# Tiles moved to SBUF places at multiples of 512 bytes, and two merge buffers made one, in a two-layer diffusion step

## Chip, core and metric

One core of a Trainium2 chip runs the whole program. The metric is the device time of one execution in microseconds (us). One execution of the kernel before was also taken by the profiler; all rows of a profile below are of that one.

## What is computed

One inference step of a small diffusion backbone with two layers, in float32. It works on 640 tokens of width 1024: 128 context tokens and 512 latent tokens (a grid of 8 x 64). Cut to what matters here:

```python
for l in range(2):
    hp = rmsnorm(xp, norm1_g[l]) * (1 + sc1p) + sh1p          # 128 context tokens
    hs = rmsnorm(xs, norm1_g[l]) * (1 + sc1s) + sh1s          # 512 latent tokens
    if l == 0:   # gated DeltaNet: projections q, k, v, z, a chunked scan both ways, w_out
        mp, ms = gdn_mixer(hp, ...), gdn_mixer(hs, ...)
    else:        # neighbourhood attention over the grid and over cached context keys, w_out
        mp, ms = context_attention(...), neighbourhood_attention(...)
    xp, xs = xp + g1p * mp, xs + g1s * ms
    xp = xp + g2p * conv_ffn(rmsnorm(xp, norm2_g[l]) * (1 + sc2p) + sh2p, ...)
    xs = xs + g2s * conv_ffn(rmsnorm(xs, norm2_g[l]) * (1 + sc2s) + sh2s, ...)
y = rmsnorm(x, final_g)

def conv_ffn(h, w_up, conv_w, conv_b, w_down):
    val, gate = split(dwconv_centred(h @ w_up, conv_w) + conv_b)   # 1024 -> 2 * 2816
    return (silu(gate) * val) @ w_down                             # 2816 -> 1024
```

The shifts, scales and gates come from `silu(c) @ w_ada + b_ada` for each layer.

## The kernel before

**Layout.** Features lie on the 128 partitions, tokens along the free dimension. The residual `X`, the normalized input of a product `hh`/`hl`, and each feature tile of the ConvFFN are rows of W = 640 float32 values, 2560 bytes per partition, the context tokens first.

**The products.** Every large product is made of three matmuls per block of 128 x 128 weights (`pass3`, L405): operand and weight are each split into a part rounded to the type float32r ("hi": `hh`, `wh`) and the rest ("lo": `hl`, `wl`), and hi·hi (L410), lo·hi (L411) and hi·lo (L412) are summed in PSUM. The moving operand is 384 columns wide, and then the other 256 (`HALVES_U`, `HALVES_R`); in the DeltaNet's projections the second part has 260 columns and begins 4 columns earlier (`HALVES_G`). A matmul with its weight load is one entry of the profile's engine PE and one of PEld. The names of the products: `dg`, `dkT`, `dqT`, `dvT`, `dzs` are the DeltaNet's projections, `rgo` its output projection, `duv` and `dug` the two halves of the up-projection, `rdn` the down-projection (its moving operand is `F`), `dqn`, `dkn`, `dvn` the attention's projections, `rne` and `rno` its output projection (its moving operand is `A`).

**The weights.** `weights` (L381) loads a chunk of weights (128 partitions x 4096 bytes for eight blocks) into one of two staging tiles `wst` by a DMA of the SyncE queue; `split` (L387) casts it on ScalarE into `wh` (L398) and subtracts on VectorE, or on GpSimd in the DeltaNet part, into `wl` (L400). `wh` and `wl` have two places each in the pool `wp`; some chunks are kept longer in places of their own.

**Order of the stages.** A start (modulation of layer 0, norm, first projections); the DeltaNet, in the order of the string `SCHED`; its output projection; the ConvFFN of layer 0, with the other modulations between its products (`ada_tile`, L154: matmuls L163 on four column groups, and L173 with a moving operand of two columns); the attention, one pair of heads after another, with the next projections between its steps; its output projection; the ConvFFN of layer 1 with the final norm. The Tile framework orders the instructions by priorities in the program and sets every wait.

**SBUF.** Tile pools are stacked: the place of a pool is the sum of the sizes of those opened before it that are still open, each tile rounded up to 32 bytes. `cst` lies lowest and holds the constants, `hh`, `hl`, the modulations and a few small tiles, some of which are allocated late in the program (`sel` at L129, `mods` at L139, `scg` at L285, `UT` and `LT` at L626, `half` at L1044). On it lies `wp` (`wst`, `wh`, `wl`), on that `gs` (small tiles of the DeltaNet), on that first the pools of the start, then `gp` (all other tiles of the DeltaNet), and when `gs` and `gp` are closed `X` and the pools of all that follows. The places before, in bytes along a partition, and the remainder by 512:

| tile | begins at | remainder by 512 |
|---|---|---|
| `hh`, `hl` | 19936, 40416 | 480 |
| `wst` (2) | 64032, 68128 | 32 |
| `wh`, `wl` (2 each) | 72224 ... 84512 | 32 |
| `X` after the DeltaNet | 88608 | 32 |
| tiles of `gp`, first `kT` | 90848 | 224 |
| `A` (8), `F` (9) | 118816 ..., 129056 ... | 32 |
| softmax tiles `P` (4) | 183456, 184960, 186464, 187968 | 160, 128, 96, 64 |

Second parts of the moving operand (256 columns) begin 1536 bytes behind the row's start, three times 512; the 260 columns begin 1520 bytes behind it, at remainder 464. A block of weights begins at a multiple of 512 bytes within its chunk, a feature row at a multiple of 2560, five times 512.

**The merge** (`merge`, L849), once for each of the eight heads, joins inverted 32 x 32 blocks: matmuls `p1`, copied to the tile `P1` by ScalarE (L880), `p2` and `p3` that read `P1`, copies back (L890, L894), `p4`, copied to `P4` (L903), `p5` that reads `P4`, and a copy back (L909). `W6`, `Wx`, `P1` and `P4` have one buffer each.

Of the kernel before, what the change touches and what calls it, by code (L numbers as in the profile page):

```python
# [12 lines left out]
F32 = mybir.dt.float32  # L13
# [13 lines left out]
NBLK = 5  # L27
# [22 lines left out]
LO0 = (1, 1, 0)  # L50
HK, HK2 = (6, 11), (2, 5)
TAB = 4
ADL, NPOOL = 1, 10
GROUPS = ((0, 8), (8, 15), (15, 22))

# [28 lines left out]
class Net:  # L84
    def __init__(self, ctx, tc, a):
        self.ctx, self.tc, self.nc, self.a = ctx, tc, tc.nc, a
        nc = self.nc
        self.cst = ctx.enter_context(tc.tile_pool(name="cst", bufs=1))
        self.lo_engine = nc.vector
        self.pd = self.pa = None  # L90
        self.wide = False
        self.hooks, self.strict = [], False
        self.chain = False
        self.pooled = None
        self.product = None
        self.wp = ctx.enter_context(tc.tile_pool(name="wp", bufs=2))
        cst = self.cst
        self.sm = cst.tile([128, NSM], F32, tag="sm", name="sm")
        nc.sync.dma_start(self.sm, a["sm"])
        self.ident = cst.tile([128, 128], F32, tag="ident", name="ident")  # L100
        make_identity(nc, self.ident)
        self.ones = cst.tile([128, 128], F32, tag="ones", name="ones")
        nc.vector.memset(self.ones, 1.0)
        self.mhalf = cst.tile([128, 8], F32, tag="mhalf", name="mhalf")
        nc.vector.memset(self.mhalf, -0.5)
        self.eps = cst.tile([128, 1], F32, tag="eps", name="eps")
        nc.vector.memset(self.eps, EPS)
        self.X = None
        self.hh = cst.tile([128, KT, W], F32R, tag="hh", name="hh")
        self.hl = cst.tile([128, KT, W], F32R, tag="hl", name="hl")  # L110
        self.cs = cst.tile([128, KT, 32], F32, tag="cs", name="cs")
        nc.vector.memset(self.cs, 0.0)
        self.mods = [None, None]
        self.scg = {}

    def open_x(self, pool):
        self.X = pool.tile([128, KT, W], F32, tag="X", name="X")
# [8 lines left out]

    def ada_begin(self):
        nc, cst = self.nc, self.cst
        self.sel = cst.tile([128, 2], F32, tag="sel", name="sel")  # L129
        nc.vector.tensor_copy(self.sel, self.ident[:, 0:2])  # L130
        for q in range(1, 4):
            nc.vector.tensor_tensor(self.sel, self.sel, self.ident[:, 32 * q : 32 * q + 2], ALU.add)
        nc.scalar.activation(
            self.cs[:, :, 0:2], self.smv("c").rearrange("p (k v) -> p k v", v=2), AF.Silu
        )
# [143 lines left out]
    def scale_vec(self, l, which, ks=range(KT)):  # L279
        nc = self.nc  # L280
        base = 8 if which == 1 else 32
        lo, hi = min(ks), max(ks) + 1
        g = self.smv("n1g" if which == 1 else "n2g").rearrange("p (l k) -> p l k", l=2)[:, l]
        if (l, which) not in self.scg:
            self.scg[l, which] = self.cst.tile([128, 8, 2], F32, tag=f"scg{l}{which}", name=f"scg{l}{which}")  # L285
        nc.vector.scalar_tensor_tensor(
            self.scg[l, which][:, lo:hi],
            self.mods[l][:, base + lo : base + hi, :],
            1.0,
            g[:, lo:hi].unsqueeze(2).to_broadcast([128, hi - lo, 2]),  # L290
            ALU.add,
            ALU.mult,
        )
# [60 lines left out]

    def norm_tile(self, np_, rs, half, k, l, which):
        nc = self.nc
        if (l, which) not in self.scg:
            self.scale_vec(l, which)
        scg = self.scg[l, which]
        base = HALVES_R[half][0]  # L360
        for hf, c0, c1, v in SEGS:
            if hf != half:
                continue
            n = c1 - c0
            t = np_.tile([128, 256], F32, tag="nt", name=f"nt{l}{which}{k}{c0}", bufs=3)
            nc.vector.scalar_tensor_tensor(
                t[:, :n], self.X[:, k, c0:c1], scg[:, k, v : v + 1], rs[:, c0 - base : c1 - base], ALU.mult, ALU.mult
            )
            sh = self.mod(l, 0 if which == 1 else 3, k, v)
            nc.scalar.activation(self.hh[:, k, c0:c1], t[:, :n], AF.Identity, bias=sh)  # L370
            nc.vector.scalar_tensor_tensor(  # L371
                self.hl[:, k, c0:c1], t[:, :n], sh, self.hh[:, k, c0:c1].bitcast(F32), ALU.add, ALU.subtract
            )
# [230 lines left out]
class Gdn:  # L604
# [17 lines left out]
    def tokens(self):  # L622

        net, nc, a = self.net, self.nc, self.net.a
        cst = net.cst
        self.UT = cst.tile([128, 128], F32, tag="UT", name="UT")  # L626
        self.LT = cst.tile([128, 128], F32, tag="LT", name="LT")
        for t, sgn in ((self.UT, 1), (self.LT, -1)):
            nc.gpsimd.affine_select(
                out=t, in_=net.ones, pattern=[[sgn, 128]], compare_op=ALU.is_ge, fill=0.0, base=0,  # L630
# [218 lines left out]
    def merge(self, h, yd, wd):  # L849
# [22 lines left out]
        def mm(out, lhsT, rhs, r, c):  # L872
            nc.tensor.matmul(out, lhsT, rhs, start=True, stop=True, tile_position=(r, c))

        p1 = self.g(f"p1{h}")
        for d, qa, qb in quads:
            for u in range(NBLK):
                mm(p1[b32(qb), u * 32 : u * 32 + 32], M[b32(qa), d, u, b32(qb)], wa[qa](u), 32 * qa, 32 * qb)
        P1 = self.gp.tile([128, NBLK, 32], F32, tag="P1", name=f"P1{h}", bufs=1)
        nc.scalar.copy(P1, p1[:, : NBLK * 32].rearrange("p (u c) -> p u c", c=32))  # L880
        p2 = self.g(f"p2{h}")
        for d, qa, qb in quads:
            for u in range(NBLK):
                mm(p2[b32(qa), u * 32 : u * 32 + 32], P1[b32(qb), u], M[b32(qb), d, u, b32(qb)], 32 * qb, 32 * qa)
        p3 = self.g(f"p3{h}")
        for d, qa, qb, o in ((0, 0, 1, 0), (1, 3, 2, 32)):
            for u in range(NBLK):
                mm(p3[b32(qb), u * 32 : u * 32 + 32], M[b32(qb), d, u, b32(qb)], P1[b32(qb), u], 32 * qb, 32 * qb)
        for d, qa, qb in quads:
# [12 lines left out]
        P4 = self.gp.tile([128, NBLK, 64], F32, tag="P4", name=f"P4{h}", bufs=1)  # L902
# [138 lines left out]

    def tokens_(self):
        net, nc = self.net, self.nc
        self.half = net.cst.tile([128, NBLK], F32, tag="half", name="half")  # L1044
        nc.vector.memset(self.half, 0.5)
        self.tokens()

# [444 lines left out]
def build(ctx, tc, a):  # L1492
# [32 lines left out]
    with tc.tile_pool(name="fp0", bufs=2, reuse_waits="tile") as fp:  # L1525
# [20 lines left out]
        def between(i):  # L1546
            if i is not None and i >= TAB:
                with net.behind([net.load]):
                    next(rows, None)
            if i is not None:  # L1550
                if joins:
                    joins.pop()()
                if direct:
                    joins.append(net.ada_tile(*direct.pop(0), fp, 1, 3, True, nxt.pop()))
                    if direct:
                        nxt.append(load())
            if calls[0] > 1:
                with net.behind([net.pooled]):
                    next(beside, None)
            calls[0] += 1  # L1560
            if i == NFT - 1:
                run(beside)
                assert not direct and not joins
# [104 lines left out]
```

## Time and profile before

| | us |
|---|---|
| median of 3 runs | 1960.89 |
| the runs | 1957.93 to 1971.5 |
| the profiled execution | 1957.87 |
| its span, from the first instruction to the last | 1955.8 |
| mean granted TensorE clock | 0.976 |

How to read it: each row of a timeline is one instruction or a run of alike ones, with its start and its duration. Matmuls are pipelined, so a row's duration is longer than the time until the next one starts; the pace of a stream is the distance from start to start, not the duration. Rows by line group the instructions of one source line; the part behind the last bar is the idle time of the engine ahead of them and what ended it.

### The profile page before, as it was taken

The numbers are of one execution on the slowest core, as the hardware profiler recorded it, in microseconds if no ns is written. First come the engines' busy times: TensorE is split into PE (matmuls) and PEld (weight loads), VectorE is DVE, ScalarE is ACT, GpSimd is POOL, SyncE is SP. The second block draws the span as 40 slices with busy tenths as digits, with TensorE's granted clock in tenths as the row PEclk, the third lists the DMA queues.
The fourth block names the chain that finished last, engine by engine and source line by source line (L and its number), as shares of the span: only waits on it lengthen the run. The fifth ranks groups of instructions, "written<-read, shape, count | busy, mean of one in ns | idle before, by whom it ended". The sixth has DMA issues, their size and how long they took to land.

```text
span 1955.8 us, 34936 instructions
## 1 busy us (share of the span) xinstructions
PE 1866.7 (95%) x14047; PEld 1762.7 (90%) x14047; DVE 1162.4 (59%) x2708; ACT 723.7 (37%) x1455; POOL 432.7 (22%) x436
## 2 busy tenths in 40 slices
PE   6889999999989999999999999999999999999998
PEld 5878888887869999999999998888889999999998
DVE  6687657767666665356446565554576643553564
ACT  4453344343334332133124344444454421331343
POOL 1332113121201828477620111111130000000000
PEclk9889899999899999999999999999999999999999
DMA  7223123323314445255233232222241322222231
GB/s 286 72 79 104 44 94 110 92 52 130 91 58 161 139 153 171 88 165 182 77 115 102 63 90 76 78 78 72 60 128 46 88 75 66 85 80 64 86 97 55
DMA packets 100835, 193.16 MB, mean 99 GB/s; under 512 B 38744, under 2 KB 58282, under 8 KB 97528
## 3 DMA queue, kind: packets, MB, share of 16 engines
q1 hardware_dynamic: 96544, 175.99, 29.0%
q0 software_dynamic: 3584, 14.40, 2.3%
q8 instruction: 111, 1.82, 0.4%
q10 hardware_dynamic: 544, 0.52, 0.1%
q14 instruction: 52, 0.43, 0.1%
HBM read 182.04 MB, written 12.46 MB: 99 GB/s over the span
## 4 chain that ended last, share of the span: by engine, by line
PE 58%; DVE 3%; issue 2%; ACT 1%; DMA 1%; POOL 0%; DVEq 0%; POOLq 0%; ACTq 0%
PE duv L410 5%; PE dug L410 5%; PE dug L411 5%; PE dug L412 5%; PE duv L411 5%; PE duv L412 5%; PE rdn L410 5%; PE rdn L412 5%; PE rdn L411 5%; PE dvn L410 1%; DMA bias<-cols 1%; PE dvn L412 1%; PE dvn L411 1%; PE dqn L410 1%; PE dqn L411 1%
## 5 line engine op out<-in xcount | busy, mean ns | idle before, releaser
L410 PE MATMUL rdn<-F,whdn 128*128 128x384 f32 (+1 forms) x704 | 218.3, 310 | 1.7 <-DVE X L476 1.7
L410 PE MATMUL duv<-hh,whuv 128*128 128x256 f32 (+1 forms) x704 | 217.6, 309 | 2.3 <-ACT yg L462 1.8
L411 PE MATMUL duv<-hl,whuv 128*128 128x256 f32 (+1 forms) x704 | 215.9, 307 | 1.8 <-DVE hl L371 1.8
L411 PE MATMUL rdn<-F,whdn 128*128 128x384 f32 (+1 forms) x704 | 217.2, 308 | 0.0
L412 PE MATMUL rdn<-F,wldn 128*128 128x384 f32 (+1 forms) x704 | 217.1, 308 | 0.0
L410 PE MATMUL dug<-hh,whug 128*128 128x256 f32 (+1 forms) x704 | 216.6, 308 | 0.0
L411 PE MATMUL dug<-hl,whug 128*128 128x256 f32 (+1 forms) x704 | 215.9, 307 | 0.0
L412 PE MATMUL dug<-hh,wlug 128*128 128x256 f32 (+1 forms) x704 | 215.9, 307 | 0.0
L412 PE MATMUL duv<-hh,wluv 128*128 128x256 f32 (+1 forms) x704 | 215.4, 306 | 0.0
L476 DVE SCALAR_TENSOR_TENSOR X<-rdn,mods,X 128x128 f32<-128x128 f32 (+1 forms) x144 | 55.0, 434 | 153.9 <-PE rdn L412 153.8
L410 PEld LDWEIGHTS duv<-hh,whuv 128*128 128x128 f32 x704 | 132.2, 188 | 7.6 <-ACT whug L398 4.5
L410 PEld LDWEIGHTS rdn<-F,whdn 128*128 128x128 f32 x704 | 133.3, 189 | 3.3 <-PE rdn L412 2.5
L411 PEld LDWEIGHTS duv<-hl,whuv 128*128 128x128 f32 x704 | 132.2, 188 | 2.6 <-DVE hl L371 2.6
L411 PEld LDWEIGHTS rdn<-F,whdn 128*128 128x128 f32 x704 | 133.3, 189 | 0.0
L412 PEld LDWEIGHTS rdn<-F,wldn 128*128 128x128 f32 x704 | 133.3, 189 | 0.0
L411 PEld LDWEIGHTS dug<-hl,whug 128*128 128x128 f32 x704 | 133.0, 189 | 0.0
L410 PEld LDWEIGHTS dug<-hh,whug 128*128 128x128 f32 x704 | 132.9, 189 | 0.0
L412 PEld LDWEIGHTS dug<-hh,wlug 128*128 128x128 f32 x704 | 132.9, 189 | 0.0
L412 PEld LDWEIGHTS duv<-hh,wluv 128*128 128x128 f32 x704 | 132.1, 188 | 0.0
L398 ACT CAST whdn<-wstdn 128x896 fp32r<-128x896 f32 (+1 forms) x48 | 47.1, 980 | 223.1 <-PE rdn L411 124.9
L331 POOL TENSOR_TENSOR nstf<-nstf,mhalf 128x3 f32<-128x3 f32 (+1 forms) x2 | 1.5, 772 | 462.0 <-DVE nstf L330 462.0
L398 ACT CAST whug<-wstug 128x1024 fp32r<-128x1024 f32 x44 | 46.1, 1048 | 139.5 <-PE dug L411 108.6
(710 smaller groups left out, 5032.4 us busy)
## 6 DMA issues: line engine op xcount, KB each, us to landing
adat<-w_ada SPq DMA_DIRECT2D x24, 1024.0 KB, 5.9
wstuv<-w_up SPq DMA_DIRECT2D x44, 512.0 KB, 3.5
wstug<-w_up SPq DMA_DIRECT2D x44, 512.0 KB, 4.1
wstdn<-w_dn SPq DMA_DIRECT2D x32, 448.0 KB, 3.3
adat<-w_ada POOLq DMA_DIRECT2D x20, 512.0 KB, 5.1
wstdn<-w_dn SPq DMA_DIRECT2D x16, 512.0 KB, 3.6
wh<-w_ada SPq DMA_DIRECT2D x14, 384.0 KB, 4.4
wl<-w_ada SPq DMA_DIRECT2D x14, 384.0 KB, 5.2
```

Source lines behind the costliest of these rows:

```text
L331: pool = nc.gpsimd.tensor_tensor(st[:, 1, :nb], st[:, 0, :nb], self.mhalf[:, :nb], ALU.pow)
L398: nc.scalar.copy(wh[:, c], st[:, c])
L410: nc.tensor.matmul(out, a, mh, start=first, stop=False)
L411: nc.tensor.matmul(out, a, ml, start=False, stop=False)
L412: ins = nc.tensor.matmul(out, b, mh, start=False, stop=last).ins
L476: nc.vector.scalar_tensor_tensor(x, ps[:, base + c0 : base + c1], self.mod(l, gi, m, v), x, ALU.mult, ALU.add)
```

## The change

`ALIGN = 32, 480` names two paddings. A tile of 32 bytes that nothing writes is allocated ahead of `hh`, and one of 480 bytes at the end of `cst`. All tiles of `cst` are now allocated when it is opened, so that its last address is known there; `UT`, `LT` and `half` go to `gs`. `P1` becomes the first 32 columns of each 64 in the one buffer of `P4`. No instruction is added or taken away in the program text.

```diff
+ALIGN = 32, 480
...
         self.X = None
+        self.align(cst, ALIGN[0])
         self.hh = cst.tile([128, KT, W], F32R, tag="hh", name="hh")
...
+        self.mods_of(0), self.mods_of(1)
+        for l in range(2):
+            for which in (1, 2):
+                self.scg[l, which] = cst.tile([128, 8, 2], F32, tag=f"scg{l}{which}", name=f"scg{l}{which}")
+        self.scaled = set()
+        self.sel = cst.tile([128, 2], F32, tag="sel", name="sel")
+        self.align(cst, ALIGN[1])
+
+    def align(self, pool, n):
+
+        if n:
+            pool.tile([128, n // 4], F32, tag=f"al{n}", name=f"al{n}")
...
-        if (l, which) not in self.scg:
-            self.scg[l, which] = self.cst.tile([128, 8, 2], F32, tag=f"scg{l}{which}", name=f"scg{l}{which}")
+        self.scaled.add((l, which))
...
-        self.UT = cst.tile([128, 128], F32, tag="UT", name="UT")
-        self.LT = cst.tile([128, 128], F32, tag="LT", name="LT")
+        self.UT = self.gs.tile([128, 128], F32, tag="UT", name="UT")
+        self.LT = self.gs.tile([128, 128], F32, tag="LT", name="LT")
...
-        P1 = self.gp.tile([128, NBLK, 32], F32, tag="P1", name=f"P1{h}", bufs=1)
+        P1 = self.gp.tile([128, NBLK, 64], F32, tag="P4", name=f"P1{h}", bufs=1)[:, :, :32]
...
-        self.half = net.cst.tile([128, NBLK], F32, tag="half", name="half")
+        self.half = self.gs.tile([128, NBLK], F32, tag="half", name="half")
```

More of the change, by code (lines that the diff above doesn't have):

```diff
@@ L128, in ada_begin @@
         nc, cst = self.nc, self.cst
-        self.sel = cst.tile([128, 2], F32, tag="sel", name="sel")
         nc.vector.tensor_copy(self.sel, self.ident[:, 0:2])
@@ L356, in norm_tile @@
         nc = self.nc
-        if (l, which) not in self.scg:
+        if (l, which) not in self.scaled:
             self.scale_vec(l, which)
@@ L624, in tokens @@
         net, nc, a = self.net, self.nc, self.net.a
-        cst = net.cst
-        self.UT = cst.tile([128, 128], F32, tag="UT", name="UT")
-        self.LT = cst.tile([128, 128], F32, tag="LT", name="LT")
+        self.UT = self.gs.tile([128, 128], F32, tag="UT", name="UT")
+        self.LT = self.gs.tile([128, 128], F32, tag="LT", name="LT")
         for t, sgn in ((self.UT, 1), (self.LT, -1)):
```

## The prediction, made before the changed kernel had run

> **What bounds the kernel now.** I read the page's first part, then the busy time by stage, then the timeline of TensorE inside a steady product, because the change moves operands and removes no work.
>
> ```profile
> span 1955.8 us, 34936 instructions
> PE 1866.7 (95%) x14047; PEld 1762.7 (90%) x14047; DVE 1162.4 (59%) x2708; ACT 723.7 (37%) x1455; POOL 432.7 (22%) x436
> ```
>
> ```profile
> core 0: us, PE busy (x) PEld busy (x) DVE busy (x) ACT busy (x) POOL busy (x), PEclk, DMA share, GB/s
> 65.00:600.00 535.00, 483.15 (x4069) 432.27 (x4068) 368.07 (x1098) 215.62 (x608) 109.36 (x82) 0.93 0.29 86
> 648.00:1122.00 474.00, 470.84 (x3414) 459.54 (x3414) 262.60 (x428) 144.36 (x176) 224.90 (x209) 1.00 0.40 127
> 1122.00:1430.00 308.00, 303.28 (x2300) 272.14 (x2299) 174.08 (x502) 135.34 (x329) 48.95 (x98) 1.00 0.25 76
> 1430.00:1492.00 62.00, 59.49 (x419) 57.37 (x418) 46.28 (x108) 30.87 (x68) 17.68 (x12) 1.00 0.31 98
> 1492.00:1956.00 464.00, 452.85 (x3140) 451.86 (x3138) 235.24 (x387) 151.93 (x188) 1.54 (x2) 0.99 0.25 77
> ```
>
> The stages are DeltaNet, ConvFFN 0, attention, its output projection, ConvFFN 1. In both ConvFFNs TensorE is busy 98 to 99% of the time, at a granted clock of 1.00 and 0.99, and VectorE only about half. There the pace of single matmuls is the time of the kernel. In the DeltaNet a tenth of the time is idle, so a faster matmul is partly swallowed by waits.
>
> Now the pace, from start to start. First `dug` from `hh` and `hl` (24 matmuls of 384 columns, then 24 of 256), then `rdn` from `F` (21 and 21), then `dvT` (15 of 260):
>
> ```profile
> 1700.31 0.33 PE L410 MATMUL dug<-hh,whug 128*128 128x384 f32 x1
> ...
> 1704.47 0.28 PE L410 MATMUL dug<-hh,whug 128*128 128x256 f32 x1
> ...
> 1707.19 0.33 PE L410 MATMUL duv<-hh,whuv 128*128 128x384 f32 x1
> ```
>
> ```profile
> 1595.10 0.34 PE L410 MATMUL rdn<-F,whdn 128*128 128x384 f32 x1
> ...
> 1598.74 0.28 PE L410 MATMUL rdn<-F,whdn 128*128 128x256 f32 x1
> ...
> 1601.25 0.34 PE L410 MATMUL rdn<-F,whdn 128*128 128x384 f32 x1
> ```
>
> ```profile
> 259.46 0.28 PE L410 MATMUL dvT<-hh,whvT 128*128 128x260 f32 x1
> ...
> 261.26 0.28 PE L410 MATMUL dvT<-hh,whvT 128*128 128x260 f32 x1
> ```
>
> 384 columns take 4.16/24 = 173.3 ns from `hh` and 3.64/21 = 173.3 ns from `F`. 256 columns take 2.72/24 = 113.3 ns from `hh` but 2.51/21 = 119.5 ns from `F`; 260 columns take 1.80/15 = 120.0 ns. Within `F`, 128 columns more cost 53.8 ns, 0.42 ns a column. At that rate 384 columns are 161.4 ns and 256 are 107.6 ns. So each matmul carries an excess: 11.9 ns for 384 columns, 11.9 ns for 256 columns of `F`, 5.7 ns for 256 columns of `hh`. The last two differ in nothing of size, weights or PSUM columns that I can find; they differ in where the moving operand begins, at remainder 32 and at remainder 480. The excess depends on the place, then. Every weight, `hh`, `hl`, `F` and `A` begins at an odd multiple of 32 bytes, so no row of a three-matmul product shows an aligned one.
>
> ScalarE shows one. The four softmax buffers lie in turn at remainders 160, 128, 96 and 64, and the same exponential runs on an odd multiple of 32 and then on a multiple of 64:
>
> ```profile
> 1175.77 0.61 ACT L1227 ACTIVATE Ps<-Ps,sts 128x376 f32<-128x376 f32 x1 [0.28 <-DVE sts L1224]
> ...
> 1176.38 0.59 ACT L1227 ACTIVATE Ps<-Ps,sts 128x376 f32<-128x376 f32 x1
> ```
>
> 0.61 against 0.59 us: about 15 to 20 ns once per instruction, near TensorE's 11.9.
>
> **The change part by part.** *The places.* 32 bytes ahead of `hh` bring it to 19968 = 39 x 512, `hl` to 40448 = 79 x 512. `UT`, `LT` and `half` leave `cst` (512 + 512 + 32), 480 + 32 come in, net 544 less: `wst` begins at 64032 - 544 = 63488 = 124 x 512, `wh` and `wl` follow in steps of 4096, `X` at 88064 = 172 x 512, `A` and `F` at remainder 0. `gs` grows by 1056, so `gp` begins at 90848 + 512 and keeps remainder 224: the DeltaNet's own tiles gain nothing. The 260 columns begin at remainder 1520 - 1024 = 496, still no multiple of 32.
>
> Counts, each row being one of the three matmuls of a product:
>
> ```profile
> L410 PE MATMUL duv<-hh,whuv 128*128 128x384 f32 x352 | 120.2, 341 | 1.8 <-ACT yg L462 1.8
> L410 PE MATMUL rdn<-F,whdn 128*128 128x256 f32 x352 | 99.6, 283 | 0.0
> L410 PE MATMUL dqn<-hh,whqn 128*128 128x384 f32 x64 | 23.7, 370 | 0.0
> L410 PE MATMUL dvT<-hh,whvT 128*128 128x384 f32 x64 | 23.5, 366 | 1.1 <-DVE vT L467 1.1
> L410 PE MATMUL rgo<-hh,whgo 128*128 128x384 f32 x64 | 21.9, 344 | 0.0
> L410 PE MATMUL rno<-A,whno 128*128 128x256 f32 x64 | 18.3, 285 | 0.0
> L410 PE MATMUL dkT<-hh,whkT 128*128 128x384 f32 x48 | 17.9, 373 | 0.0
> L410 PE MATMUL rne<-A,whne 128*128 128x384 f32 x32 | 11.5, 358 | 0.0
> L410 PE MATMUL rno<-A,whno 128*128 128x384 f32 x32 | 10.9, 341 | 1.3 <-ACT whno L398 1.3
> L410 PE MATMUL dg<-hh,whg 128*128 128x384 f32 x24 | 9.1, 378 | 0.0
> ```
>
> The aligned pace is unknown. Its two ends: unchanged, and the bare column rate. A weight load could hold it up; its nearest row is a matmul of two columns behind a full weight load, four of them in 0.43 us, 107.5 ns each, so 107.6 for 256 columns just fits:
>
> ```profile
> 674.68 0.50 PE L173 MATMUL adp<-sel,adev 128*128 128x2 f32 x4
> 675.11 0.41 PE L163 MATMUL adp<-wl,cs 128*32 128x256 f32 x2
> ```
>
> I take the bare rate, since the ScalarE row, the only one with both kinds of place, loses about the whole excess. The 260 columns I leave at 120 (ends: 120 and 109.2).
>
> ConvFFNs: 9 x 352 matmuls of 384 columns x 11.9 ns = 37.7 us; 6 x 352 of 256 from `hh` x 5.7 = 12.0; 3 x 352 from `F` x 11.9 = 12.6; together 62.3 us, all on the path. Output projections: (64 + 32 + 32) x 3 x 11.9 = 4.6, 192 x 5.7 = 1.1, 192 x 11.9 = 2.3; 8.0, of which I count 7.2, as the first lies partly in the DeltaNet's tail. Attention's projections: 9 x 64 x (11.9 + 5.7) = 10.1 us; the other steps there wait for transfers of the bias (below), so half, 5.0. DeltaNet: (48 + 3 x 64 + 24) x 3 = 792 x 11.9 = 9.4; a third, 3.1. Sum 77.6 us.
>
> ```profile
> POOL bias L1206 <- DMA bias<-cols: 77.3, 30, 4.5
> ```
>
> By the Trainium skill (page "TensorE: Matmul & The Clock Gate", section "Back-to-back issue gap") a lone stream of N columns should be spaced by N/2.4 + 2.5 ns. That is 162.5 and 109.2, which no row of a three-matmul product here reaches; with these the estimate would be 67 us instead.
>
> *What the faster matmuls call for.* Two up-projections take 24 x (173.3 + 113.3) x 2 = 13.8 us now and would take 12.9. Behind them lie two loads, casts and subtractions:
>
> ```profile
> L400 DVE TENSOR_TENSOR wlug<-wstug,whug 128x1024 fp32r<-128x1024 f32 x42 | 57.9, 1380 | 56.2 <-ACT whug L398 56.1
> L398 ACT CAST whug<-wstug 128x1024 fp32r<-128x1024 f32 x44 | 46.1, 1048 | 139.5 <-PE dug L411 108.6 <-PE rdn L411 22.2 <-DMA wstug<-w_up 5.6
> wstug<-w_up SPq DMA_DIRECT2D x44, 512.0 KB, 4.1
> ```
>
> 4.1 + 1.0 + 1.4 = 6.5 us against 12.9 for a buffer's turn: covered; the casts wait for TensorE (108.6 us) and hardly for the DMA (5.6). Aligned staging and casts may get shorter, behind the same cover: 0. Were the cover gone, a chunk would show up to its 6.5 us.
>
> *The shared buffer.* ScalarE may write the next head's `P1` only when `p5` has read `P4`, and `P4` only when `p3` has read `P1`.
>
> ```profile
> 182.05 1.20 PE L873 MATMUL p<-M,P 64*64 64x64 f32 x20 [0.52 <-ACT P L903]
> ```
>
> ```profile
> 198.76 0.29 ACT L880 COPY P<-p 128x160 f32<-128x160 f32 x1 [0.78 <-PE p L873]
> ```
>
> The reads end at 183.25, the next write starts 15.5 us later, and within a head `p4` needs the copies behind `p3` anyway. Cost 0; without the cover seven heads x 1.2 us = 8.4 us at worst, with ScalarE's queue behind the copy. The earlier allocations and the two paddings issue nothing.
>
> **Sum.** 1957.9 (the profiled execution) - 77.6 = 1880.3. That execution lies 3.0 us under the median of the runs shown, so I add 2: **1882 us**.
>
> **Rivals.** *Half of it.* If the excess comes in steps of about 6 ns, as 5.7 against 11.9 suggests, alignment may take one step only: 6.0 for 384 and for `F`, 5.7 for `hh`. ConvFFNs 4224 x 6.0 + 2112 x 5.7 = 37.4, output projections 4.1, attention 3.4, DeltaNet 1.6: 46.5, so 1911 + 2 = 1913. For it: equal excess of 384 columns at both places. Against it: ScalarE's row.
>
> *Nothing.* The excess belongs to four-byte streams of this width, and a multiple of 32 is as good as any: 1958 to 1961. For it: 384 columns pace alike at remainders 480 and 32. Against it: 113.3 against 119.5 for the same 256 columns. The Trainium skill (page "SBUF — State Buffer", section "Specifications (TRN2)") gives SBUF lines of 16 bytes; by that rule all places are aligned already and nothing changes. ScalarE's row, slower at a multiple of 32 than at one of 64, speaks against that.
>
> *Slower.* What counts is the distance between the moving operand and the weights that load meanwhile. `F` and its weights share remainder 32 and pace at 119.5; `hh` at 480 and weights at 32 pace at 113.3. Afterwards all share remainder 0, and 256 columns of `hh` go to 119.5: 6.2 x (2112 + 192 + 576/2) = 16.1 us, so 1974 + 2 = 1976. It decides as soon as that pace rises above 113.3 while the others stay. Against it: 260 columns at remainder 464, far from the weights' 32, are slow too.
>
> *It doesn't do what it says*, or the planner orders something differently after the merge of the buffers: a few us either way.
>
> **How the numbers follow.** Forecast 0.52, half 0.20, nothing 0.15, slower 0.10, the rest 0.03. About 1% of 1958, 20 us, is what a measurement here can tell from no change. Faster by over 1%: 0.52 + 0.20 + 0.01 = 0.73. Within 1%: nothing, 0.05 of the slower case (16 us is 0.8%) and 0.01 of the rest, 0.21. Slower by over 1%: 0.06. The low end takes the attention's and the DeltaNet's sums in full and the 260 columns at 109.2 (5.1 + 6.3 + 8.6 more): about 1862. The high end takes in half and most of nothing: 1959. The forecast's own range is 1862 to 1900.
>
> **What would show it.** Right: 384 columns pace at 161 to 163 ns and both kinds of 256 at 108 to 110 in the timeline of `dug` and `rdn`; ConvFFN 1 is 30 us shorter; 260 columns still 120; DMA and casts as before. Half: 167 and 108 to 114. Wrong: 173.3 unchanged, 256 columns of `hh` at 119.5, or the idle time of TensorE in the ConvFFNs growing by what the matmuls gained.

## The result, and the profile after

The changed kernel takes 1973.8 us at the median (17 runs, 1963.9 to 1985.7), the kernel before in the same comparison 1959.9 us (17 runs). The ratio is 1.0076, with a 95% interval of 1.0054 to 1.0098: slower by 11 to 19 us. The profiled execution after has a span of 1971.0 us against 1955.8, 15.2 us more. (Of all the executions below one, of 2071 us at a granted clock of 0.93, is left out of its ratio; it belongs to the kernel with `F` and `A` moved.)

First the head of the page of the changed kernel, then its busy time by stage (columns as before: stretch, length, PE, PEld, DVE, ACT and POOL busy with counts, granted clock, DMA share, GB/s).

```profile
span 1971.0 us, 34940 instructions
PE 1884.1 (96%) x14047; PEld 1780.7 (90%) x14047; DVE 1162.0 (59%) x2708; ACT 724.3 (37%) x1455; POOL 431.3 (22%) x436
```

```profile
65.00:600.00 535.00, 484.29 (x4070) 433.98 (x4070) 367.99 (x1098) 216.35 (x608) 109.49 (x82) 0.93 0.28 86
648.00:1122.00 474.00, 471.02 (x3363) 459.59 (x3362) 259.61 (x418) 140.34 (x167) 220.70 (x207) 1.00 0.40 127
1492.00:1971.00 479.00, 468.90 (x3202) 468.00 (x3200) 241.30 (x403) 155.59 (x196) 2.25 (x3) 0.99 0.24 74
```

The reader sees three things. TensorE is busy 17.4 us longer (1884.1 against 1866.7) with the same 14047 matmuls; VectorE, ScalarE and GpSimd are busy as long as before to within 1.4 us, and every engine's count of busy instructions is the same (the page's total of 34940 is four above that of before). In the same 474 us of ConvFFN 0, TensorE stays as full as it was but gets 3363 matmuls done where it did 3414. And the DeltaNet's stretch is the same. So no wait appeared: the matmuls themselves became slower.

Which ones, the timeline of TensorE inside a steady product shows (start, duration, line, operands; one of the three matmuls of each product). The lines moved down by 12: L410 of before is L422 here.

```profile
1713.12 0.34 PE L422 MATMUL dug<-hh,whug 128*128 128x384 f32 x1
...
1717.28 0.28 PE L422 MATMUL dug<-hh,whug 128*128 128x256 f32 x1
...
1720.15 0.34 PE L422 MATMUL duv<-hh,whuv 128*128 128x384 f32 x1
```

```profile
1606.94 0.34 PE L422 MATMUL rdn<-F,whdn 128*128 128x384 f32 x1
...
1610.59 0.28 PE L422 MATMUL rdn<-F,whdn 128*128 128x256 f32 x1
...
1613.10 0.34 PE L422 MATMUL rdn<-F,whdn 128*128 128x384 f32 x1
```

384 columns from `hh` still take 4.16/24 = 173.3 ns, from `F` 3.65/21 = 173.8. 256 columns from `F` still take 2.51/21 = 119.5. But 256 columns from `hh`, 113.3 ns before, now take 2.87/24 = 119.6. Of the streams of 384 and 256 columns only the fastest changed, and it became like the others. 6.3 ns x (2112 + 192 + 288) = 16 us is about the whole difference of the spans.

By stage, from the first matmul of its first large product to that of the next stage's, before and after: ConvFFN 0 495.5 and 501.2 us, attention 272.2 and 274.2, its output projection 74.7 and 76.1, ConvFFN 1 (to its last product) 463.9 and 469.7; the DeltaNet's last product starts its last matmul at 518.3 and 518.2 us.

Both traces have the same 14047 matmuls in the same order, so that each can be set beside its like. The later start of the changed kernel grows by 5.7 us over the up-projections of ConvFFN 0 and by 5.9 us over those of ConvFFN 1, and by nothing over the down-projections between them. The output projection's 1.4 us are not of this kind: they come in some ten matmuls near 1465 us, where the changed kernel's execution was granted a clock of 0.50.

### The profile page after: what moved, and what is told of

It is laid out like the page before. It is cut to its first block, busy times and chain, and to the rows that moved or that the text cites. A ratio compares the mean times of both kernels' runs of the same rounds, so it can differ in the third digit from the quotient of the medians.

```text
span 1971.0 us, 34940 instructions
## 1 busy us (share of the span) xinstructions
PE 1884.1 (96%) x14047; PEld 1780.7 (90%) x14047; DVE 1162.0 (59%) x2708; ACT 724.3 (37%) x1455; POOL 431.3 (22%) x436
## 4 chain that ended last, share of the span: by engine, by line
PE 59%; DVE 3%; issue 2%; ACT 1%; DMA 1%; POOL 0%; DVEq 0%; POOLq 0%; ACTq 0%
PE duv L422 5%; PE dug L422 5%; PE dug L423 5%; PE dug L424 5%; PE duv L423 5%; PE duv L424 5%; PE rdn L422 5%; PE rdn L423 5%; PE rdn L424 5%; PE dvn L422 1%; DMA bias<-cols 1%; PE dvn L424 1%; PE dvn L423 1%; PE dqn L422 1%; PE dqn L424 1%
## 5 line engine op out<-in xcount | busy, mean ns | idle before, releaser
L422 PE MATMUL duv<-hh,whuv 128*128 128x256 f32 (+1 forms) x704 | 219.4, 312 | 1.9 <-DVE yv L479 1.4
L422 PE MATMUL rdn<-F,whdn 128*128 128x384 f32 (+1 forms) x704 | 218.3, 310 | 1.7 <-DVE X L488 1.7
L422 PE MATMUL dug<-hh,whug 128*128 128x256 f32 (+1 forms) x704 | 218.4, 310 | 0.0
L422 PEld LDWEIGHTS duv<-hh,whuv 128*128 128x128 f32 x704 | 133.3, 189 | 7.1 <-ACT whug L410 4.4
L422 PEld LDWEIGHTS rdn<-F,whdn 128*128 128x128 f32 x704 | 133.3, 189 | 3.3 <-PE rdn L424 2.5
L422 PEld LDWEIGHTS dug<-hh,whug 128*128 128x128 f32 x704 | 133.8, 190 | 0.0
L410 ACT CAST whdn<-wstdn 128x896 fp32r<-128x896 f32 (+1 forms) x48 | 47.0, 978 | 221.6 <-PE rdn L423 124.3
L410 ACT CAST whug<-wstug 128x1024 fp32r<-128x1024 f32 x44 | 46.2, 1049 | 145.6 <-PE dug L423 113.0
```

The costliest lines, as they stand in the source:

```text
L410: nc.scalar.copy(wh[:, c], st[:, c])
L422: nc.tensor.matmul(out, a, mh, start=first, stop=False)
```

## The experiments

The theory after this result: the pace of a three-matmul product depends on the **distance** in SBUF between what streams and the weights, not on the place of either (A). `hh` at 480 and weights at 32 gave 113.3; everything at 0 gives 119.6, as `F` and its weights at 32 did before. The main rival: the place of the **moving operand alone** counts (B); 480 is good, 0 and 32 are bad.

### Streams alone, 16 x 16 places

```
def stream(n, r, w):
    for k in range(8):
        m = [mov[:, i * 5120 + k * W + r // 4 :][:, :n] for i in range(2)]
        b = [wts[:, i * 2048 + k * 128 + w // 4 :][:, :128] for i in range(2)]
        for x, y, z in ((0, 0, 0), (0, 1, 1), (1, 0, 2)):
            nc.tensor.matmul(ps[:, :n], b[x], m[y], start=(k == 0 and z == 0), stop=(k == 7 and z == 2))
```

> A stream of TensorE products alone: three fp32r matmuls per 128x128 weight block as in the kernel, for each of 16 places of the moving operand (0, 32, ... 480 over a multiple of 512) with each of 16 places of the weights, 256 columns; then 384 columns and a few other widths. All the rest of the computation is left out and the outputs are zeros. Theory A (the distance between moving operand and weights sets the pace): the pace of 256 columns is the same along each diagonal of the table, 120 ns at distance 0, 113 at distance 448 (480 with 32). Theory B (the place of the moving operand alone): the pace changes between the rows of the moving place only, 113 ns at 480 and 120 at 0 and 32, whatever the weights' place. Theory C (the places do not count; something else in the kernel, transfers or other engines' accesses, made the 113): one pace all over the table. 384 columns: 173 at every place for B as for A, since 0, 32 and 480 did not differ.

The granted clock was 1.00 throughout, and nothing else ran. The timeline joins equal instructions, so that a row gives start, length and count of a run of them; less the last matmul's 0.28 us and divided by the count less one it gives the pace. Four streams of 256 columns: moving operand at 192 and weights at 0; 480 and 32; 0 and 64; 480 and 480.

```profile
60.80 2.78 PE L114 MATMUL s<-mov,wts 128*128 128x256 f32 x23
131.54 2.78 PE L114 MATMUL s<-mov,wts 128*128 128x256 f32 x23
134.27 2.87 PE L114 MATMUL s<-mov,wts 128*128 128x256 f32 x23
765.91 2.92 PE L114 MATMUL s<-mov,wts 128*128 128x256 f32 x23
```

The first two have the distances 192 and 448 and the same pace, 2.50/22 = 113.6 ns. The third has the distance -64, which is 192 modulo 256 too, and yet 117.7 ns: it is the first stream behind a change of the weights' place, of which more below. Further on, where the weights are at 352 and the moving operand at 288, the same distance of -64 has 113.7. The fourth has distance 0 and 120.0. Median paces along the diagonals, from the starts of the matmuls:

```
distance modulo 256      0     32     64     96    128    160    192    224
256 columns, ns      119.7  118.0  118.0  119.6  118.7  117.4  113.7  118.0
384 columns, ns      174.5  173.3  173.4  176.6  176.2  176.7  174.7  174.3
```

Every row of the 16 x 16 table holds these same values, shifted along with the weights' place and repeating every 256 bytes, apart from the first streams of a row, up to six, behind the change of the weights' place. At distance 192, 24 streams of 256 columns have 113.7 ns, and the eight among those first ones 114.7 to 117.8. So A holds and B and C fall. 384 columns have no place with an excess near zero: nothing in the table is below 173.2 ns, and the 161.4 of the prediction is never approached.

### Everything at 480, and `hh` at 0 with the weights at 64

```
-ALIGN = 32, 480
+ALIGN = 0, 480      # first kernel: all at remainder 480
+ALIGN = 32, 32      # second: hh, hl at 0; weights, staging, X, A, F at 64
```

> The changed kernel with no padding ahead of hh: hh, hl, staging, weights, residual, A and F all begin at remainder 480. A (distance): all distances are 0 as in the changed kernel, 256 columns of hh at 120 ns, time as the changed kernel, 1974 us. B (place of the moving operand): 256 columns of hh back at 113.3 and those of F and A at 113.3 too; 1248 x 6.2 ns = 7.7 us below before, 1952 us. If places do not count: 1960 to 1974 without a pattern by place.

> The changed kernel with the second padding 32 instead of 480: hh and hl at remainder 0, weights, staging, residual, A and F at 64, so the distance from hh to its weights is 448 as before. A: 256 columns of hh at 113.3, of F at 120: time as before, 1960. B: 256 columns of hh at 120 as in the changed kernel; F at 64 unknown: 1974 if 64 is like 0 and 32, 1967 if it is like 480.

The first: 1969.3 us against 1957.8 before, ratio 1.0061 (1.0041 to 1.0081). The second: 1957.5 us, ratio 1.0001 (0.9979 to 1.0023). Their timelines, in this order:

```profile
1705.36 0.34 PE L422 MATMUL dug<-hh,whug 128*128 128x384 f32 x1
1709.53 0.28 PE L422 MATMUL dug<-hh,whug 128*128 128x256 f32 x1
1712.39 0.34 PE L422 MATMUL duv<-hh,whuv 128*128 128x384 f32 x1
```

```profile
1709.42 0.33 PE L422 MATMUL dug<-hh,whug 128*128 128x384 f32 x1
1713.58 0.28 PE L422 MATMUL dug<-hh,whug 128*128 128x256 f32 x1
1716.30 0.33 PE L422 MATMUL duv<-hh,whuv 128*128 128x384 f32 x1
```

With `hh` at its old 480 but the weights there too, 256 columns take 2.86/24 = 119.2 ns. With `hh` at its new 0, a multiple of 512, and the weights 64 further on, they take 2.72/24 = 113.3. B would have had it the other way round. A holds in the kernel as it did in the streams.

### The shared merge buffer alone

```
-        P1 = self.gp.tile([128, NBLK, 32], F32, tag="P1", name=f"P1{h}", bufs=1)
+        P1 = self.gp.tile([128, NBLK, 64], F32, tag="P4", name=f"P1{h}", bufs=1)[:, :, :32]
```

> The kernel before with the shared merge buffer alone, all places of hh, weights, F and A as before. Theory of the shared buffer costing nothing: 1960 and a DeltaNet that ends at the same time. Rival, the sharing costs waits: up to 8.4 us in the DeltaNet, 1968.

1957.4 us, ratio 0.9994 (0.9970 to 1.0017). The sharing costs nothing that can be measured. The waits of ScalarE ahead of its two copies (total us, times, longest us), the first pair of the kernel before, the second of the changed one:

```profile
ACT P L903 <- PE p L873: 27.8, 8, 6.8
ACT P L880 <- PE p L873: 17.1, 8, 5.2
```

```profile
ACT P L914 <- PE p L884: 28.1, 8, 6.8
ACT P L891 <- PE p L884: 17.1, 8, 5.2
```

They are the waits for the product that is to be copied, and they are unchanged (26.4 and 19.0 us in the run with the shared buffer alone); none for the buffer has come in.

### Steps of 4 bytes, separate places, narrower weights

```
ORDER += [(n, r, r, 0, 0) for r in range(0, 260, 4)]              # width, hh, hl, wh, wl
ORDER += [(n, 0, s, 0, s) for s in range(0, 256, 16)]             # hl and wl moved together
ORDER += [(n, r, r, 0, 0, 128, c) for r in range(0, 256, 32)]     # c = 96, 64, 32 columns of weights
```

> Streams of TensorE products alone, as in the first table; all the rest of the computation is left out and the outputs are zeros. The first table gave one pace along each diagonal, so the distance counts, and only modulo 256 bytes: 113.7 ns at 192, 119.7 at 0. Here the distance goes in steps of 4 bytes, hh's and hl's part and wh's and wl's part are moved separately, and the weight block gets fewer columns or rows. Theory A1 (each matmul streams while the weights of the NEXT one load, and the distance between those two counts): with the second moving operand AND the second weights both moved by s, every pair that runs together has distance 0, so all s give 119.7; with the second moving operand alone at 192 only every third matmul, the one that streams it, is shorter, by 18 ns in all over three if the whole gain of 6 ns sits in it, mean 117.7. Rival A2 (the distance to the matmul's OWN weights, which are already loaded): both moved by 192 gives distances 0, 192 and 64 and a mean near 117. Theory D (the two reads collide, and what is lost is the loading's doing): weight blocks of 64 or 32 columns lose less than 13 ns, and the distance counts less. Rival E (a fixed cost of each matmul of this type, plus a small effect of the place): 384 columns stay at 173 with 32 columns of weights. For 384 columns the table had 173.3 to 176.7; a step of 4 bytes may show a better place, or none.

Paces from the starts of the matmuls, in ns:

```
equal distances, steps of 4:  256 columns 113.3 (at 16 and 144; 114.0 at 192) to 122.8 (at 84)
                              384 columns 173.1 (at 64) to 180.5 (at 180)
hl and wl both moved by s:    256 columns 120.1 at s = 192, 117.8 at 64, 117.1 to 120.0 at the others
hl alone at 192:              256 columns 118.0, 117.3, 118.0 for the three matmuls, mean 117.8
weights of 32 columns:        256 columns 113.5 to 117.8; 384 columns 173.1 to 175.6
weights of 64 rows:           256 columns 113.4 to 119.9; 384 columns 173.3 to 176.8
```

D falls for 384 columns: over the eight distances from 0 to 224 they take 174.1 ns in the mean with 128 columns of weights and with 32, though the load itself is much shorter. At 256 columns the means are 117.8 and 115.8 ns, so there the narrower load is worth 2 ns. The weight loads of 128 and of 32 columns (busy us, mean ns):

```profile
L114 PEld LDWEIGHTS s<-mov,wts 128*128 128x128 f32 x7152 | 1053.3, 189 | 35.1 <-ACT mov L99 18.2
...
L114 PEld LDWEIGHTS s<-mov,wts 128*32 128x32 f32 x384 | 41.4, 108 | 14.2
```

189 against 108 ns of loading. E holds for 384 columns: the least pace at equal distances is 173.1 ns (171.1 with `hl` alone elsewhere), some 13 ns above 384 columns at the 0.416 ns each that bfloat16 shows further below, (215.8 - 109.2)/256. At 256 columns the least, 113.3, is 7 ns above them, so that here the place makes more of the excess than E has it. Between A1 and A2 it settles nothing. 120.1 at s = 192 is A1's value, but 117.8 at s = 64 is not; and with `hl` alone moved the mean is what A1 gave, but all three matmuls have it, not the one that streams `hl`.

### Which weights, and another type

```
wr = s * (i % 2)                          # weights in turn at 0 and s
mr = ((wr if own else s - wr) + d) % 256  # moving operand: distance d to its own, or to the next weights
```

> Streams of 48 single matmuls; all the rest of the computation is left out and the outputs are zeros. The weights lie in turn at remainder 0 and 128, and the moving operand follows so that either its distance to its OWN weights is fixed at d (and the one to the NEXT weights is d + 128), or the distance to the NEXT weights is d (and to its own d + 128). The plain tables gave 256 columns 113.7 to 114 ns at 192 and 117.8 at 64, 384 columns 173.3 at 112 and 180.0 at 240. Theory A1 (the weights that load meanwhile count): next 192 gives 113.7 and own 192 gives 117.8; next 112 gives 173.3 and own 112 gives 180. Rival A2 (the matmul's own weights): the other way round. If both give a middle value in both forms, neither pair alone counts, but the pattern of the whole stream. The same streams in bfloat16, at distances 0 to 224: if the 13 ns that every fp32r matmul carries above its columns belong to four-byte operands, bfloat16 gives 107 to 110 ns for 256 columns and 160 to 163 for 384 at every distance; if they belong to any stream with weight loads, 113 to 120 and 173 again.

256 columns: 116.6 to 116.7 ns in every form with the weights in turn at 0 and 128. Neither pair alone counts, but the pattern of the whole stream, as the third case of the expectation has it. 384 columns brought a surprise. "Own 240" and "next 112", two names of one list of matmuls, take 185.4 ns, slower than any stream with its weights at one place; neither A1 nor A2 has such a value. "Own 112" and "next 240" are one and the same list too, yet the first takes 176 and the second 170 ns, in each of three repetitions; and the plain stream of 256 columns at distance 192 took 113.5 ns at first and 117.8 where it stood behind a stream of 384. The rows, each from inside one stream; first 384 columns, "own 112" and "next 240", then 256 columns at distance 192 at the two places:

```profile
91.73 8.28 PE L120 MATMUL s<-mov,wts 128*128 128x384 f32 x46
117.98 8.00 PE L120 MATMUL s<-mov,wts 128*128 128x384 f32 x46
```

```profile
41.42 5.05 PE L120 MATMUL s<-mov,wts 128*128 128x256 f32 x43
126.50 5.23 PE L120 MATMUL s<-mov,wts 128*128 128x256 f32 x43
```

(8.28 - 0.34)/45 = 176.4 against 170.2 ns; (5.05 - 0.28)/42 = 113.6 against 117.9. So the pace also depends on **what streamed before**, and equal instructions can settle differently. Some of the values lie 3.3 ns apart (113.3, 116.7, 120.0; 170.0, 173.3, 176.7, 180.0), others between, such as 117.8.

Even the same predecessors don't fix it. The kernel with the shared merge buffer alone has the 14047 matmuls of the kernel before in the same order, with `hh`, `hl` and all weights at the same places; yet in the first 16 up-products of ConvFFN 1 its 256 columns of `hh` settle, from the third on, at 117.8 ns where the kernel before has 113.4, and are back at 113.4 in the next group. One product of the kernel before, and the same one of the kernel with the shared buffer:

```profile
1537.33 0.28 PE L410 MATMUL dug<-hh,whug 128*128 128x256 f32 x1
...
1540.06 0.33 PE L410 MATMUL duv<-hh,whuv 128*128 128x384 f32 x1
```

```profile
1536.04 0.28 PE L410 MATMUL dug<-hh,whug 128*128 128x256 f32 x1
...
1538.86 0.34 PE L410 MATMUL duv<-hh,whuv 128*128 128x384 f32 x1
```

2.73/24 = 113.8 against 2.82/24 = 117.5 ns. At distance 192 a stream of 256 columns thus runs mostly at one of two paces, 113.4 and 117.8 ns. What chooses between them is not shown.

bfloat16, 256 and 384 columns, from inside two streams, and the mean durations of their matmuls:

```profile
327.92 4.86 PE L127 MATMUL s<-mb,wb 128*128 128x256 bf16 x43
...
338.50 7.31 PE L127 MATMUL s<-mb,wb 128*128 128x384 bf16 x44
```

```profile
L127 PE MATMUL s<-mb,wb 128*128 128x384 bf16 x384 | 62.6, 326 | 0.0
L127 PE MATMUL s<-mb,wb 128*128 128x256 bf16 x384 | 42.1, 273 | 0.0
```

(4.86 - 0.273)/42 = 109.2 and (7.31 - 0.326)/43 = 162.4 ns, and by the starts 109.2, 162.5 and (512 columns) 215.8 at all eight distances. The bfloat16 streams have neither float32r's excess (162.5 against at least 170.0 ns) nor a dependence on the place. By the Trainium skill (page "TensorE: Matmul & The Clock Gate", section "Back-to-back issue gap") the gap of a lone matmul of N columns is N/2.4 + 2.5 ns, which gives 109.2, 162.5 and 215.8; for a stream with weight loads it has about 131 ns at 512 columns. The bfloat16 streams here have a weight load each and agree with the formula to the tenth, not with the 131; float32r never came down to the formula.

### `F` and `A` moved to distance 192

```
+                    if i == 0:
+                        fp.tile([128, 48], F32, tag="pad0", name=f"pad0{l}", bufs=1)
                     f = fp.tile([128, 2 * W], F32R, tag="F", name=f"F{l}{i}", bufs=9).rearrange("p (a w) -> p a w", a=2)
+                    if i == 0:
+                        fp.tile([128, 16], F32, tag="pad1", name=f"pad1{l}", bufs=1)
```

The same stands around `A`. The second kernel does it to the changed one, and begins `hh` and `hl` 192 bytes into their tiles.

> The kernel before with F and A moved by 192 bytes, from 32 to 224 modulo 256, by a padding of 192 ahead of their buffers and 64 behind them; hh, hl and the weights stay. The distance from F and A to the weights goes from 0 to 192, that of hh stays 192. Theory (the tables of single streams carry over): 256 columns of F and A go from 119.5 to 113.5 ns, 384 columns stay at 173 to 175; 1248 x 6.0 = 7.5 us less, 1950. Rival (the streams of the kernel have another sequence, or other engines' accesses count): no change, 1958.

> The changed kernel with hh, hl, F and A moved by 192 bytes and the weights left at multiples of 512: all distances 192. Theory (distance alone): all 256 columns at 113.5, time as the kernel before with F and A moved, 1950; the changed kernel is mended and more, and that the weights begin at multiples of 512 is worth nothing. Rival (aligned weights are worth something once the distance is right): below 1945. Rival (the place of the moving operand counts by itself): 1974.

Kernel before with `F` and `A` moved: 1957.9 us against 1959.6, ratio 0.9994 (0.9973 to 1.0016). Changed kernel with all at 192: 1956.0 us, ratio 0.9987 (0.9965 to 1.0008). The first one's timeline:

```profile
1597.44 0.28 PE L410 MATMUL rdn<-F,whdn 128*128 128x256 f32 x1
...
1599.82 0.33 PE L410 MATMUL rdn<-F,whdn 128*128 128x384 f32 x1
```

2.38/21 = 113.3 ns: where it is shown the stream has the pace that the theory gives. Over the whole kernel it has not. Mean paces at full clock inside the products, in ns:

```
                                     before   F, A at 192   after, all at 192
F 256, ConvFFN 0 / 1           119.5 / 119.5  114.2 / 115.4     114.7 / 115.3
F 384, ConvFFN 1                        173.6         174.0             174.0
hh 256, ConvFFN 1                       113.5         114.9             114.9
A 256                                   119.9         113.5             117.4
```

For `F` and `A` moved alone that is 528 x (5.3 + 4.1) + 192 x 6.4 = 6.2 us gained and 1056 x 1.4 + 528 x 0.4 = 1.7 us given back by streams whose distance did not change: 4.5 us, where I had 7.5; the interval allows 5.3 us of gain at most and does not exclude none. Product by product it is the two paces of distance 192 again: of 38 unbroken streams of 256 columns from `F`, 26 run at 113 to 114 ns and 12 at 118. The 1.4 ns that `hh` gave back are one group of up-products at 117.8; the kernel with the shared buffer has the same mean, 114.9, with neither `F` nor `A` moved, so this is not shown to be the moving's doing. The mended form of the change is level with the kernel before, so the loss of 0.76% is gone, and aligned weights are worth nothing that can be measured once the distance is right.

### `hh` at one of the worst distances

```
-        self.hh = cst.tile([128, KT, W], F32R, tag="hh", name="hh")
+        self.hh = cst.tile([128, KT * W + 64], F32R, tag="hh", name="hh")[:, 45 : 45 + KT * W].rearrange(
+            "p (k w) -> p k w", w=W
+        )
```

The same for `hl`; `hh` then begins at 148 modulo 256, with the weights at 32.

> The kernel before with hh and hl moved so that their distance to the weights is 116 modulo 256, among the slowest of the table for both widths (256 columns 121.7 ns, 384 columns 180.0, against 113.7 and about 173.5 at 192). Theory (the table carries over): (2112 + 192) x (8.0 + 6.5) = 33.4 us in the ConvFFNs and the output projection, 4.2 in attention, 1.7 in the DeltaNet, together 39 us: about 1997. Rival (only the distance 192 is special, all others cost 6 ns for 256 columns and nothing for 384): 1974. The copies that write hh get an odd place too; if that slows them, it shows in ScalarE's and VectorE's rows, not in the pace.

1992.3 us, ratio 1.0190 (1.0151 to 1.0229), 30 to 45 us.

```profile
1708.53 0.34 PE L414 MATMUL dug<-hh,whug 128*128 128x384 f32 x1
...
1712.85 0.28 PE L414 MATMUL dug<-hh,whug 128*128 128x256 f32 x1
...
1715.73 0.34 PE L414 MATMUL duv<-hh,whuv 128*128 128x384 f32 x1
```

384 columns take 4.32/24 = 180.0 ns, as the stream alone had it, and 256 take 2.88/24 = 120.0 instead of 121.7. By stage: ConvFFN 0 507.6 us, attention 277.5, ConvFFN 1 477.4; 12.1, 5.2 and 13.5 more than before. 39 us lies within the interval; the rival's 16 does not. The table carries over to the kernel.

### All 512 combinations in the kernel's sequence

```
for rh in range(0, 256, 32):
    for rl in range(0, 256, 32):
        for wl in range(0, 256, 32):
            ORDER += [(n, rh, rl, 0, wl) for n in (384, 256)]
```

> Streams of products alone in the kernel's own sequence (24 matmuls of 384 columns, then 24 of 256, over three matmuls per weight block), for all 512 combinations in steps of 32 bytes of the places of hh, hl and wl against wh; all the rest of the computation is left out and the outputs are zeros. So far the best pair is 173.3 + 113.3 = 286.6 ns, which the kernel before has for hh. Theory P (the pattern of the whole stream sets the pace, in steps of 3.3 ns; a stream of 384 at 170.0 was seen with weights in turn at two places): some combination gives 280 to 284 for the pair, and a kernel placed so saves up to (2112 + 192) x 4 = 9 us on hh. Rival F (equal distance of all three matmuls is the best that there is, mixed places only average): none is below 286, most lie at 291 to 294 (173.3 to 176 + 117.8). If a combination that was measured before (all at 0, all at 192) comes out another way here, the pace depends on what streamed before as well.

Sums of the two paces, in ns: best 286.7 (`hh` and `hl` at 192, `wl` at 128), next 288.7 (`hh` and `hl` at 192, `wl` at 0, the arrangement of the kernel before), median 293.4, worst 300.0; all at 0, the arrangement of the change, 293.0. F holds: nothing is below 286. The kernel before has 173.3 + 113.3 for `hh`, as good as the best of 512, though its own arrangement came to 288.7 here: what a stream settles into moves a sum by as much as the places at the top of the list differ. No placement was found that beats it by more than the comparison can tell.

## Why the prediction was wrong

**The step that failed** is the pace: "I take the bare rate, since the ScalarE row, the only one with both kinds of place, loses about the whole excess." Behind it stands "The excess depends on the place, then." Of the two widths and three streams, none came to the bare rate. That rate, 161.4 and 107.6 ns, was worked out from the two widths of `F` alone; the bfloat16 streams, the fastest here, have 162.5 and 109.2.

- *384 columns.* Predicted 173.3 to 161.4 ns; measured 173.3. The streams alone give 173.1 as the least of 64 distances. The 11.9 ns that I took for a loss of place are lost by float32r matmuls at every equal distance that was tried, to within a few tenths (173.1 - 161.4 = 11.7); bfloat16 has 162.5 at this width. That `hh` at 480 and `F` at 32 paced alike at 384 columns was in the quoted rows, and it was the evidence for this.
- *256 columns of `F` and `A`.* Predicted 119.5 to 107.6; measured 119.5, since their distance to the weights stayed 0.
- *256 columns of `hh`.* Predicted 113.3 to 107.6; measured 119.6. The two streams that I compared differ "in where the moving operand begins", I wrote, and left out the other half of the same observation: in one of them the weights shared its remainder, in the other they did not. I had this reading as the rival and priced it at 16.1 us; I set it at 0.10.
- *ScalarE as the nearest row.* The exponential's 0.61 and 0.59 us are no matter of the place at all. In the changed kernel the softmax tiles lie 544 bytes lower, at remainders 128, 96, 64 and 32, so that the first exponential of a pair now has the multiple of 64 and the second the odd multiple of 32. The first is still the slower, 611 against 595 ns in the mean of 16 pairs, as before (610 and 595):

```profile
1182.41 0.61 ACT L1238 ACTIVATE Ps<-Ps,sts 128x376 f32<-128x376 f32 x1 [0.28 <-DVE sts L1235]
...
1183.02 0.59 ACT L1238 ACTIVATE Ps<-Ps,sts 128x376 f32<-128x376 f32 x1
```

The two rows that were compared differed in their turn within the pair as well, and the 16 ns go with that turn. So the reason given for the bare rate, which was also held against the rivals *Half* and *Nothing*, was none.

- *The sum.* ConvFFNs: -62.3 us predicted; +5.7 and +5.8 by stage. Output projections and attention: -12.2 predicted; +1.1 for the DeltaNet's output projection (120.6 us before), +1.9 for the attention, and +1.4 for the attention's output projection, where nearly all of it is the granted clock's. DeltaNet: -3.1 predicted; unchanged. The 260 columns, which I had left at 120, went to 118.7 (fifteen of `dvT` from 259.67 to 261.45 us), as the streams alone have it at their new places, 118.7 for 496 and 0 against 120.3 for 464 and 32.

**Right** were the terms at nothing. The shared buffer costs nothing (shown alone). The cover of loads and casts holds; in the changed kernel:

```profile
L412 DVE TENSOR_TENSOR wlug<-wstug,whug 128x1024 fp32r<-128x1024 f32 x42 | 57.7, 1375 | 61.0 <-ACT whug L410 61.0
L410 ACT CAST whug<-wstug 128x1024 fp32r<-128x1024 f32 x44 | 46.2, 1049 | 145.6 <-PE dug L423 113.0 <-PE rdn L423 22.2 <-DMA wstug<-w_up 7.0
wstug<-w_up SPq DMA_DIRECT2D x44, 512.0 KB, 3.9
```

Casts take 1049 ns (1048 before), subtractions 1375 (1380), loads 3.9 us (4.1): the aligned places of the staging did nothing for them either. Right was also where the time would move, in the ConvFFNs' pace with TensorE full, and right in size, and in its mechanism as far as the distance goes, was the rival that I called *Slower*: 1976 us and 119.5 ns, against 1973.8 and 119.6. That the distance is to the weights "that load meanwhile" the runs do not show. Its counter-evidence, the slow 260 columns far from the weights' place, was weak, for 260 columns take 118 to 121 ns at every distance in the streams alone.

The rival *Nothing* had a true half. Most of the excess does belong "to four-byte streams of this width", as far as float32r was tried; but not every multiple of 32 is as good as any other. By the Trainium skill (page "SBUF — State Buffer", section "Specifications (TRN2)") SBUF has lines of 16 bytes, by which the rival took all places to be equal; here places that are all multiples of 32 gave 113.3 and 119.6 ns.

**Open** stays why the distance counts and only modulo 256, which of the weights it is to be taken to, and what makes equal streams at equal places settle at one pace or another. Read from the traces is only the pace.

## What to carry to other kernels

An operand's place cost the float32r matmuls of this kernel 1.9% at one of the worst distances (1959.6 to 1992.3 us with nothing else changed), but what counts is its distance to the weights modulo 256 bytes, and equal alignment of both, the tidy choice, is among the worse ones for 256 columns. Before an excess is called removable, look whether any row shows it removed for the same engine, type and width; if none does, measure a stream of that instruction alone, which settles it. And where two rows differ in pace, list everything in which they differ, the second operand's place and the turn within a pair included, before one of the differences is made the cause. A trace of the changed kernel can then test the reading: here it moved the softmax tiles too.

## What the runs showed that I had not expected

- At 0.416 ns a column, a float32r matmul stream at equal distances carries 13 to 21 ns above its columns for 384 (173.1 to 180.5 ns) and 7 to 16 for 256 (113.3 to 122.8), and with weights of 32 columns still 13 and 7 at the least; a bfloat16 stream 2.6 ns, at every place.
- Place and list don't fix its pace: the same list of matmuls of 384 columns ran at 176.4 and at 170.2 ns, three times each, by what stood before it, and 256 columns of `hh` ran at 113.4 or 117.8 ns in two kernels with the same matmuls, order and places.
- The pace repeats every 256 bytes of distance, and steps of 4 bytes move it by up to 9 ns (256 columns: 113.3 ns at 16, 122.3 at 20; 384 columns: 173.3 at 112, 180.0 at 116).
